# Grouping the sampled tokens' state updates by array rows, and moving one gate product and the later weight casts, in a two-layer hybrid decoder

## Chip, cores and metric

One Trainium2 chip, one core. The metric is the device time of one launch in microseconds (us), as the median of several runs. The launch computes the whole model step.

## The reference

Two decoder layers, float32, over 512 prompt tokens and 8 samples of 4 tokens (544 token columns), model width 1024. Each layer is a half-step SwiGLU FFN, a mixer, cross attention and a second FFN. The mixer is what the change touches. It projects the normalised input once and feeds two groups of heads: sliding-window attention (8 query heads, 2 key heads) and gated linear attention (GLA; 4 heads, key width 64, value width 128). Cut to GLA:

```python
def step(S, inp):                       # one chunk of 64 tokens (4 for a sample)
    b = cumsum(gate); b_last = b[-1]
    q_t, k_t = q * exp(b), k * exp(-b)
    o = q_t @ S + where(causal, q_t @ k_t.T, 0) @ v
    S_new = exp(b_last)[:, None] * S + (k * exp(b_last - b)).T @ v
# per head: rms_norm(o) * silu(g), g one more block of the projection
mix = concat(window_attention, gla) @ w_out
```

The 8 samples each have a state of 4 x 64 x 128 that is read, updated by `S_new`, and written out.

## The kernel before

Tokens lie along the free axis: every activation is 128 features by 544 tokens. A product with a 1024-wide weight block ("block") takes a slab of 128x1024 from HBM into `raw` (3 buffers), and `weights` (L209) splits it into `hi`, a cast on ScalarE (L213), and `lo`, a subtraction on VectorE (L214); `hi` has 3 buffers, `lo` 2. `product` (L221) then issues 48 matmuls at L230 into one of two `pm` tiles of two PSUM banks. All other PSUM results share four one-bank `pa` tiles (`psa`).

The mixer (L676) is a set of Python generators, and the string `MIX` (L52) lists in what order they are advanced, one part at a time. The tile framework then orders the instructions of each engine itself: the place in `MIX` is a priority, and an instruction whose inputs and tiles are there may go earlier. All DMAs are issued by SyncE (SP), in order. Names in `MIX`:

- `rot 0..4`: key and query blocks of the window attention. Part 1 is the block and `taken` (L406), which copies the result (L409) and squares it (L410) into a temporary `u` (3 buffers). Part 2 swaps partition halves by four DMAs into a `z` (L987) and rotates it on VectorE (L988 to L990).
- `qf`: `row_sums` (L264) of the four query squares: matmuls at L272, copies to a `z` at L275, transposes at L278; then the query factors (L258 to L261), which the softmax exponentials (L578) need.
- `gla 0..3`: 128 prompt tokens each. Part 1 makes scores and states, part 2 the outputs (L863 to L873), part 3 is `normed` (L794): squares with sums (L801), square root (L805, "root" below), reciprocal, two products (L809), four transposes (L814) and the copy to `bt` (L815).
- `glas`: the same for the samples. `states`: their state updates. For two samples at a time it masks `kst` (32 sample tokens by 256) into `kdm` (L943, [32, 256]), multiplies `kdm` with the values `vgs` (L948, 32 rows of the array, 64 of its columns), and adds the decayed state (L954); four parts.
- `gated 0..3`: the gate blocks; part 1 the block and its scaling into a `z` (L388), part 2 `silu` (L1028) and product with `bt` (L1029). `bparts` splits the gated result for the output blocks `out 1 x`; `out 0 x` uses the window attention.
- `score n w`, `vals n`, `swas`: window attention. `sv`: its value block.

`z` has 6 buffers (`ATT`, L47), shared by all of these. The order of `MIX` around the change is, before:

```python
"... rot 4, glas, states, rot 3, gla 3, rot 4, gla 3, qf, qf, score 1 0, states, score 0 0, gated 0, sv, "
"score 1 0, states, score 0 1, score 1 1, score 1 0, gated 2, score 0 0, ... gated 1, ... gated 3, ..."
```

Of the kernel before, what the change touches and what calls it, by code (L numbers as in the profile page):

```python
# [7 lines left out]
F32 = mybir.dt.float32  # L8
# [11 lines left out]
NB = 8  # L20
# [33 lines left out]
    "rot 0, gate, key 0, query 1, value 2, query 0, key 1, qdecay 1, value 3, kdecay 1, value 3, kdecay 1, kdecay "  # L54
    "0, sv, value 2, value 0, rot 0, kdecay 0, qdecay 0, value 1, value 0, value 1, gla 0, gla 1, glas, gla 0, "
    "gla 1, gla 2, rot 1, gla 0, gla 2, glas, rot 2, gla 1, gated 0, gla 3, rot 2, rot 1, rot 3, gla 2, rot 4, "
    "glas, states, rot 3, gla 3, rot 4, gla 3, qf, qf, score 1 0, states, score 0 0, gated 0, sv, score 1 0, "
# [5 lines left out]
)  # L63
CROSS = (
    "keys, xq 0, keys, keys, xq 1, xq 2, xq 3, factors, mvalues, mvalues, score 0, xbd, score 1, mvalues, "
# [19 lines left out]
def decoder_kernel(  # L85
# [87 lines left out]
    def hv(t):  # L173
        return t.rearrange("p (a n) -> p a n", a=2)

    fetched = []

    def load(l, i):
        raw = wp.tile([128, 1024], F32, tag="raw", bufs=BUFS["raw"], name="raw")
# [29 lines left out]
    def weights(l, i):  # L209
        raw = ready.pop(0) if ready else load(l, i)  # L210
        hi = wp.tile([128, 1024], F32R, tag="hi", bufs=BUFS["hi"], name="hi")
        lo = wp.tile([128, 1024], F32R, tag="lo", bufs=BUFS["lo"], name="lo")
        act.copy(out=hi, in_=raw)  # L213
        dve.tensor_tensor(out=lo, in0=raw, in1=hi.bitcast(F32), op=ALU.subtract)  # L214
        return hi, lo

    def split(src, hi, lo):
# [185 lines left out]
    def halves():  # L403
        return [slice(0, HN), slice(HN, N)]

    def taken(ps, g, dst):  # L406

        sq = tmp("u")
        act.activation(out=hv(dst), in_=ps[:, :, :HN], func=AF.Copy, scale=g)  # L409
        act.activation(out=hv(sq), in_=ps[:, :, :HN], func=AF.Square)  # L410
        return sq
# [269 lines left out]
    def mixer(l, nx, nxt):  # L681
# [21 lines left out]
        qk = big()  # L703
        q_t, k_t = [qk[:, 0, :], qk[:, 1, :]], [qk[:, 2, :], qk[:, 3, :]]
        ktok = lay.tile([128, 4, 256], F32, tag="ktok", name="ktok")
        kst = lay.tile([32, 256], F32, tag="w1", name="kst")
        ends = lay.tile([128, 2, 16], F32, tag="ends", name="ends")
        def key(i):
            block(2 + i, k_t[i])
# [33 lines left out]

        vg = big()
        vgt = vg.rearrange("p a b -> p (a b)")[:, 0:2048].rearrange("p (n h c) -> p n h c", n=4, h=4)
        vgs = lay.tile([32, 4, 128], F32, tag="vgs", name="vgs")
        def value(h):
            z = tmp("z")
            block(4 + h, z)
            yield 1  # L750
            ps = psa()
            for n in range(4):
                pe.transpose(ps[:, n * 128:n * 128 + 128], z[:, n * 128:n * 128 + 128], ident)
            act.copy(out=vgt[:, :, h, :], in_=ps.rearrange("p (n c) -> p n c", n=4))
            ps = psa()
            pe.transpose(ps[0:32, 0:128], z[:, T:N], ident)
            act.copy(out=vgs[:, h, :], in_=ps[0:32, 0:128])

        def query_decay(i):
            e = tmp("u")  # L760
# [3 lines left out]
        def key_decay(i):  # L764
            e, d = tmp("u"), tmp("u")
            c = cum[i]
            cp, cs = c[:, 0:T].rearrange("p (c t) -> p c t", t=64), c[:, T:N].rearrange("p (c t) -> p c t", t=NT)
            dve.tensor_tensor(
                out=d[:, 0:T].rearrange("p (c t) -> p c t", t=64), in0=cp,
                in1=cp[:, :, 63:64].to_broadcast([128, 8, 64]), op=ALU.subtract,  # L770
            )
            dve.tensor_tensor(
                out=d[:, T:N].rearrange("p (c t) -> p c t", t=NT), in0=cs,
                in1=cs[:, :, NT - 1:NT].to_broadcast([128, NB, NT]), op=ALU.subtract,
            )
            act.activation(out=d, in_=d, func=AF.Exp, scale=-1.0 / 16)
            act.activation(out=ends[:, i, 0:8].unsqueeze(2), in_=cp[:, :, 63:64], func=AF.Exp, scale=1.0 / 16)
            act.activation(out=ends[:, i, 8:16].unsqueeze(2), in_=cs[:, :, NT - 1:NT], func=AF.Exp, scale=1.0 / 16)
            dve.tensor_tensor(out=d, in0=d, in1=k_t[i], op=ALU.mult)
            act.activation(out=e, in_=c, func=AF.Exp, scale=-1.0 / 16)  # L780
            dve.tensor_tensor(out=k_t[i], in0=k_t[i], in1=e, op=ALU.mult)
            yield 1
            ps = psa()
            for n in range(4):
                pe.transpose(ps[:, n * 128:n * 128 + 128], d[:, n * 128:n * 128 + 128], ident)
            act.copy(out=ktok[:, :, i * 128:i * 128 + 128], in_=ps.rearrange("p (n c) -> p n c", n=4))
            ps = psa()
            pe.transpose(ps[0:32, 0:128], d[:, T:N], ident)
            act.copy(out=kst[:, i * 128:i * 128 + 128], in_=ps[0:32, 0:128])

        bt = big()
        gain = col[:, l, C_ON:C_ON + 1]
# [1 line left out]
        def normed(os, c0):  # L794

            sm = smp.tile([128, 4, 4], F32, tag="sm", name="sm")
            su = sm[:, 0, :]
            z = tmp("z")[:, 0:T].rearrange("p (i e v) -> p e i v", e=2, i=2)
            for e in range(2):
                for i in range(2):  # L800
                    act.activation(  # L801
                        out=z[:, e, i, :], in_=os[e][:, i, :], func=AF.Square,
                        accum_out=su[:, 2 * i + e:2 * i + e + 1],
                    )
            act.activation(out=su, in_=su, func=AF.Sqrt, scale=1.0 / 128, bias=eps)  # L805
            dve.reciprocal(out=su, in_=su)
            f = su.rearrange("p (i e) -> p e i", e=2)
            for e in range(2):
                dve.tensor_tensor(  # L809
                    out=z[:, e], in0=os[e], in1=f[:, e].unsqueeze(2).to_broadcast([128, 2, 128]), op=ALU.mult  # L810
                )
            ps = psa().rearrange("p (h t) -> p h t", h=4)
            for h in range(4):
                pe.transpose(ps[:, h, :], z[:, h % 2, h // 2, :], ident)  # L814
            act.activation(out=bt[:, :, c0:c0 + 128], in_=ps, func=AF.Copy, scale=gain)  # L815
# [65 lines left out]
        def gla_sample():  # L881
            sv = s0[l].rearrange("b (i h) d v -> (h d) b i v", i=2)
            st0 = []
            for g in range(2):
                t = cache().rearrange("p (b i v) -> p b i v", b=4, i=2)
                for i in range(2):
                    nc.sync.dma_start(out=t[:, :, i, :], in_=sv[:, 4 * g:4 * g + 4, i, :])
                st0.append(t)
# [18 lines left out]
            for h in range(4):  # L907
                r = slice(32 * h, 32 * h + 32)
                pe.matmul(
                    o[r, :], ams[:, 2 * (h % 2) + h // 2, :], vgs[:, h, :], start=True, stop=False,  # L910
                    tile_position=(0, 32 * h),
                )
            for b in range(NB):
# [20 lines left out]
        def gla_states():  # L934
            st0 = held["st0"]
            osv = o_ss[l].rearrange("b (i h) d v -> (h d) b i v", i=2)
            for b in range(0, NB, 2):
                if b:
                    yield 1
                up = psa().rearrange("p (b i v) -> p b i v", b=2, i=2)  # L940
                for e in range(2):
                    kdm = lay.tile([32, 256], F32, tag="kdm", name="kdm")
                    dve.tensor_scalar(  # L943
                        out=kdm, in0=kst, scalar1=kc[0:32, K_BAT + b + e:K_BAT + b + e + 1], scalar2=None, op0=ALU.mult
                    )
                    for h in range(4):
                        rows = slice(64 * (h % 2), 64 * (h % 2) + 64)
                        pe.matmul(  # L948
                            up[rows, e, h // 2, :], kdm[:, 64 * h:64 * h + 64], vgs[:, h, :], start=True, stop=True
                        )  # L950
                for e in range(2):
                    for i in range(2):
                        t = st0[b // 4][:, (b + e) % 4, i, :]
                        dve.scalar_tensor_tensor(  # L954
                            out=t, in0=t, scalar=ends[:, i, 8 + b + e:9 + b + e], in1=up[:, e, i, :],
                            op0=ALU.mult, op1=ALU.add,
                        )
            for g in range(2):
                for i in range(2):
                    nc.sync.dma_start(out=osv[:, 4 * g:4 * g + 4, i, :], in_=st0[g][:, :, i, :])  # L960
# [6 lines left out]
        def rotated(i):  # L967
            dst = kt if i == 0 else qt[:, i - 1, :]
            g = col[:, l, C_KN:C_KN + 1] if i == 0 else col[:, l, C_QN:C_QN + 1]
            sq = taken(raw_block(8 + i), g, dst)  # L970
            if i == 0:
                ps = psa()[:, 0:10].rearrange("p (b h) -> p b h", b=5)
                by_token(ps, 0, sq, sum_k)
# [75 lines left out]
        def output(half, q):  # L1049
            hh, hl = ((ah, al), (bh, bl))[half]  # L1050
            hi, lo = weights(l, SL_OUT + 4 * half + q)
            for i in range(2):
# [7 lines left out]
                ])  # L1060
                residual(ps, 2 * q + i, 1.0, None if half else nxt)

        run(MIX, dict(
            key=key, gate=gate, query=query, value=value, qdecay=query_decay, kdecay=key_decay, gla=gla_prompt,
            glas=gla_sample, states=gla_states, rot=rotated, qf=query_factors, sv=swa_value, gated=gated,
# [448 lines left out]
```

## Time and profile before

| | us |
|---|---|
| median of 3 runs | 2187.13 (2184.15 to 2187.5) |
| the profiled execution | 2186.87 |
| its span, first to last instruction | 2184.7 |
| TensorE busy in the span | 2165.0 (99%) |
| VectorE busy | 1566.5 (72%) |
| ScalarE busy | 1048.0 (48%) |

The span is what the trace covers; the time has 2.17 us around it. The profile is read by engine: PE is TensorE's matmuls, DVE VectorE, ACT ScalarE, SPq SyncE's queue of DMA issues. The two layers run the same program with other weights; the first layer's mixer runs from about 365 to 617 us, the second's lies 1080 us later.

### The profile page before, as it was taken

Reading aid. Unit: us, or ns where it says so; the run is one execution under the profiler, and the core shown is the slowest. Engines: PE = TensorE matmul, PEld = TensorE weight load, DVE = VectorE, ACT = ScalarE, POOL = GpSimd, SP = SyncE. Lnnn points to the kernel's source line nnn. Section 1 sums busy time; section 2 is a strip of 40 time slices with the busy share of each in tenths; the row PEclk is TensorE's granted clock in tenths of the full one; section 3 lists DMA queues with packets and bytes.
Section 4 is the critical chain, followed back from the end, with each engine's and each line's share of the span. In section 5 each row is a group of like instructions: output and inputs, shape, how many; then the busy total and the mean of one; then the engine's idle time right before and its main releaser. Section 6 shows DMA issues by size and latency. Waiting matters only on the chain.

```text
span 2184.7 us, 40872 instructions
## 1 busy us (share of the span) xinstructions
PE 2165.0 (99%) x17306; PEld 2092.8 (96%) x17306; DVE 1566.5 (72%) x2471; ACT 1048.0 (48%) x1721; POOL 7.0 (0%) x17
## 2 busy tenths in 40 slices
PE   9999999999999999999999999999999999999999
PEld 9999999997897999999999999999879979999999
DVE  6986876547754898777688787765477458977774
ACT  6544443536455644444454444445455466444441
POOL 0000000000000000000000000000000000000000
PEclk9999999999999999999999999999999999999999
DMA  4323333222345232232233323332232533233232
GB/s 141 110 93 98 116 97 130 88 86 73 96 134 195 85 111 96 87 109 95 78 97 99 105 88 92 104 129 90 74 91 88 202 118 105 90 109 93 87 107 71
DMA packets 74998, 227.07 MB, mean 104 GB/s; under 512 B 7712, under 2 KB 19744, under 8 KB 73504
## 3 DMA queue, kind: packets, MB, share of 16 engines
q1 hardware_dynamic: 74816, 224.47, 32.1%
q8 instruction: 135, 2.21, 0.4%
q14 instruction: 47, 0.39, 0.1%
HBM read 214.64 MB, written 9.04 MB: 102 GB/s over the span
## 4 chain that ended last, share of the span: by engine, by line
PE 94%; DVE 3%; DMA 2%; ACT 1%; issue 0%; SPq 0%; ACTq 0%; DVEq 0%
PE pm L230 47%; PE pa L461 36%; PE pa L230 1%; PE pm L1152 1%; PE pm L1114 1%; PE pa L1254 1%; PE pa L1284 1%; PE pm L1237 0%; DMA raw<-in_wts_dram 0%; PE pa L606 0%; PE pm L556 0%; PE pa L239 0%; DMA big<-in_cmv_dram 0%; PE pa L590 0%; PE pa L272 0%; DVE big L219 0%
## 5 line engine op out<-in xcount | busy, mean ns | idle before, releaser
L230 PE MATMUL pm<-big,hi 128*128 128x272 f32 x5632 | 781.3, 290 | 3.4 <-DVE big L219 0.8
L230 PEld LDWEIGHTS pm<-big,hi 128*128 128x128 f32 x5632 | 733.7, 189 | 12.1 <-issue 2.9
L230 PE MATMUL pm<-big,lo 128*128 128x272 f32 x2816 | 410.4, 289 | 0.0
L230 PEld LDWEIGHTS pm<-big,lo 128*128 128x128 f32 x2816 | 374.5, 188 | 2.1 <-issue 1.2
L213 ACT CAST hi<-raw 128x1024 fp32r<-128x1024 f32 x196 | 205.5, 1048 | 241.5 <-PE pm L230 133.0
L214 DVE TENSOR_TENSOR lo<-raw,hi 128x1024 fp32r<-128x1024 f32 x196 | 238.5, 1217 | 51.4 <-PE pm L230 29.7
L218 ACT CAST hs<-sum 128x1024 fp32r<-128x1024 f32 x152 | 160.0, 1053 | 172.1 <-PE pa L461 125.3
L461 PE MATMUL pa<-t,hs 128*128 128x272 f32 x1368 | 238.6, 288 | 0.0
L461 PE MATMUL pa<-big,hs 128*128 128x272 f32 x1064 | 211.2, 288 | 0.1
L461 PEld LDWEIGHTS pa<-t,hs 128*128 128x128 f32 x1368 | 200.9, 188 | 0.0
L219 DVE TENSOR_TENSOR ls<-sum,hs 128x1024 fp32r<-128x1024 f32 x152 | 185.1, 1218 | 1.9 <-ACT hs L218 1.0
L461 PE MATMUL pa<-big,hi 128*128 128x272 f32 x1216 | 178.9, 289 | 0.0
L399 DVE SCALAR_TENSOR_TENSOR x<-pm,x 128x544 f32<-128x544 f32 x192 | 138.1, 719 | 48.1 <-PE pm L230 48.0
L461 PEld LDWEIGHTS pa<-big,hs 128*128 128x128 f32 x1064 | 166.5, 188 | 0.4 <-DVE big L219 0.4
L461 PEld LDWEIGHTS pa<-big,hi 128*128 128x128 f32 x1216 | 163.0, 188 | 0.0
L461 PE MATMUL pa<-t,ls 128*128 128x272 f32 x912 | 152.9, 289 | 0.0
L461 PEld LDWEIGHTS pa<-t,ls 128*128 128x128 f32 x912 | 129.7, 188 | 0.0
L218 ACT CAST hi<-raw 128x1024 fp32r<-128x1024 f32 x76 | 80.1, 1054 | 90.2 <-PE pm L230 81.1
L218 ACT CAST hd<-raw 128x512 fp32r<-128x512 f32 x76 | 47.2, 621 | 137.7 <-PE pa L461 127.6
L447 DVE TENSOR_TENSOR sum<-raw 128x512 f32<-128x512 f32 x152 | 98.2, 686 | 18.0 <-DMA raw<-in_wts_dram 17.6
L461 PE MATMUL pa<-big,lo 128*128 128x272 f32 x608 | 109.6, 288 | 0.0
L447 DVE TENSOR_TENSOR sum<-sum,raw 128x512 f32<-128x512 f32 x152 | 103.9, 684 | 0.0
(306 smaller groups left out, 2611.2 us busy)
## 6 DMA issues: line engine op xcount, KB each, us to landing
raw<-in_wts_dram SPq DMA_DIRECT2D x348, 512.0 KB
big<-in_cmk_t_dram SPq DMA_DIRECT2D x8, 1024.0 KB
big<-in_cmv_dram SPq DMA_DIRECT2D x8, 1024.0 KB
kc<-in_consts_dram SPq DMA_DIRECT2D x2, 1546.0 KB
x<-in_x_dram SPq DMA_DIRECT2D x8, 272.0 KB
z<-big SPq DMA_DIRECT2D x32, 68.0 KB
out_dram<-x SPq DMA_DIRECT2D x8, 272.0 KB
cache<-in_s_dram SPq DMA_DIRECT2D x8, 256.0 KB
```

The costliest lines, as they stand in the source:

```text
L213: act.copy(out=hi, in_=raw)
L214: dve.tensor_tensor(out=lo, in0=raw, in1=hi.bitcast(F32), op=ALU.subtract)
L218: act.copy(out=hi, in_=src)
L219: dve.tensor_tensor(out=lo, in0=src, in1=hi.bitcast(F32), op=ALU.subtract)
L230: pe.matmul(half_of(ps, h, s.stop - s.start), w, x[:, s], start=i == 0, stop=i == len(steps) - 1)
L399: dve.scalar_tensor_tensor(out=x, in0=p, scalar=scale, in1=x, op0=ALU.mult, op1=ALU.add)
L447: dve.tensor_tensor(out=t[:, e], in0=t[:, 0] if x is None else x, in1=y, op=ALU.add)
L461: pe.matmul(ps, u, v, start=first and i == 0, stop=i == len(steps) - 1, skip_group_check=not first)
L1114: pe.matmul(pk[:, h, :], w[:, o:o + 128], x[:, k, :], start=st and h % 2 == 0, stop=sp and h % 2 == 1)
L1152: pe.matmul(pv[:, c, :], x[:, k, c * 128:c * 128 + 128], w[:, o], start=st, stop=sp)
L1254: pe.matmul(o[:, h * 128:h * 128 + 128], held["mv"][:, c, h * 128:h * 128 + 128], pts[:, (2 * e + c) * 128:(2 * e + c + 1) * 128], start=c ...
L1284: pe.matmul(o[32 * e:32 * e + 32, :], pts[:, (2 * g + c) * 128 + 32 * e:(2 * g + c) * 128 + 32 * e + 32], vt[e // 2][:, e % 2, c, :], star ...
```

## The change

- `kst` and `vgs` get 128 rows. SBUF-to-SBUF DMAs copy their 32 rows to the other three groups of 32 rows (six DMAs a layer), and `own_tok`, loaded by four small DMAs a layer, has in row group j the mask of samples j and j+4.
- `states` masks twice instead of eight times, all four row groups at once, into a `z`; its 32 products are the same but lie in four row groups of the array; it has two parts instead of four, and holds two `pa` tiles in each.
- In `MIX`, `gated 2`'s block goes in ahead of the third part of `gla 3`; `gated 1` and `gated 3` each move up one place; `rot 3` and `rot 4`'s second parts come after `gla 3`; `bparts` comes earlier.
- `rot 4`'s square goes into a `z` instead of a `u`.
- `weights` issues the casts of every slab that is traced after `gla 3`'s third part behind that part's root (ACT) and second product (DVE). The edge orders instructions within an engine and adds no semaphore.

```diff
-    "glas, states, rot 3, gla 3, rot 4, gla 3, qf, qf, score 1 0, states, score 0 0, gated 0, sv, score 1 0, "
-    "states, score 0 1, score 1 1, score 1 0, gated 2, score 0 0, score 0 1, score 0 0, score 2 0, score 0 1, "
-    "score 1 1, vals 0, swas, gated 1, score 2 1, score 1 1, gated 1, gated 2, gated 3, score 3 1, vals 1, score "
-    "3 1, score 2 0, score 2 1, score 2 1, states, swas, score 2 0, bparts, vals 2, bparts, score 3 0, score 3 0, "
-    "bparts, gated 3, bparts, out 1 3, out 1 3, out 1 0, swas, ...
+    "glas, gla 3, states, gated 2, gla 3, rot 3, rot 4, qf, qf, score 1 0, score 0 0, gated 0, sv, score 1 0, states, "
+    "score 0 1, score 1 1, score 1 0, gated 1, score 0 0, score 0 1, score 0 0, score 2 0, score 0 1, score 1 1, vals "
+    "0, swas, gated 3, score 2 1, score 1 1, gated 1, gated 2, gated 3, score 3 1, vals 1, score 3 1, bparts, score 2 "
+    "0, bparts, score 2 1, score 2 1, bparts, swas, score 2 0, bparts, vals 2, out 1 3, score 3 0, score 3 0, out 1 "
+    "3, out 1 0, swas, ...
...
-    fetched = []
+    fetched, fence = [], []
...
-        act.copy(out=hi, in_=raw)
-        dve.tensor_tensor(out=lo, in0=raw, in1=hi.bitcast(F32), op=ALU.subtract)
+        with ExitStack() as behind:
+            for ins in fence:
+                behind.enter_context(tc.issue_after(ins))
+            act.copy(out=hi, in_=raw)
+            dve.tensor_tensor(out=lo, in0=raw, in1=hi.bitcast(F32), op=ALU.subtract)
...
-    def taken(ps, g, dst):
-        sq = tmp("u")
+    def taken(ps, g, dst, tag="u"):
+        sq = tmp(tag)
...
-        kst = lay.tile([32, 256], F32, tag="w1", name="kst")
+        kst = lay.tile([128, 256], F32, tag="w1", name="kst")
...
-        vgs = lay.tile([32, 4, 128], F32, tag="vgs", name="vgs")
+        vgs = lay.tile([128, 4, 128], F32, tag="vgs", name="vgs")
+        own_tok = lay.tile([128, 2], F32, tag="own", name="own_tok")
+        for j in range(4):
+            nc.sync.dma_start(out=own_tok[32 * j:32 * j + 32, :], in_=consts[0:32, K_BAT + j:K_BAT + NB:4])
...
-            act.activation(out=su, in_=su, func=AF.Sqrt, scale=1.0 / 128, bias=eps)
+            root = act.activation(out=su, in_=su, func=AF.Sqrt, scale=1.0 / 128, bias=eps)
...
-                dve.tensor_tensor(
+                mult = dve.tensor_tensor(
...
+            if c0 == 384:
+                fence[:] = [root.ins, mult.ins]
...
+            for j in range(1, 4):
+                own = slice(32 * j, 32 * j + 32)
+                nc.sync.dma_start(out=kst[own, :], in_=kst[0:32, :])
+                nc.sync.dma_start(out=vgs[own, :, :], in_=vgs[0:32, :, :])
...
-            for b in range(0, NB, 2):
-                if b:
+            z = tmp("z")
+            kdm = [z[:, 256 * g:256 * g + 256] for g in range(2)]
+            for g in range(2):
+                dve.tensor_scalar(
+                    out=kdm[g], in0=kst, scalar1=own_tok[:, g:g + 1], scalar2=None, op0=ALU.mult
+                )
+            for j0 in (0, 2):
+                if j0:
                     yield 1
-                up = psa().rearrange("p (b i v) -> p b i v", b=2, i=2)
-                for e in range(2):
-                    kdm = lay.tile([32, 256], F32, tag="kdm", name="kdm")
...
+                up = [psa().rearrange("p (g i v) -> p g i v", g=2, i=2) for _ in range(2)]
+                for g in range(2):
+                    for i in range(2):
+                        for j, u in enumerate(up, start=j0):
+                            own = slice(32 * j, 32 * j + 32)
+                            for e in range(2):
+                                h = 2 * i + e
+                                pe.matmul(
+                                    u[64 * e:64 * e + 64, g, i, :], kdm[g][own, 64 * h:64 * h + 64], vgs[own, h, :],
+                                    start=True, stop=True,
+                                )
+                for j, u in enumerate(up, start=j0):
+                    for g in range(2):
+                        for i in range(2):
+                            t = st0[g][:, j, i, :]
...
-            sq = taken(raw_block(8 + i), g, dst)
+            sq = taken(raw_block(8 + i), g, dst, "z" if i == 4 else "u")
...
+        fence[:] = []
         run(MIX, dict(
```

## Rows read from the trace of the kernel before

**Rows 1.** The page, its first line and part 1, the line of PE.

```profile
span 2184.7 us, 40872 instructions
...
PE 2165.0 (99%) x17306; PEld 2092.8 (96%) x17306; DVE 1566.5 (72%) x2471; ACT 1048.0 (48%) x1721; POOL 7.0 (0%) x17
```

**Rows 2.** Waits of PE, whole span: us in total, times, longest.

```profile
PE pa L814 <- DVE z L809: 4.3, 2, 2.1
...
PE pa L272 <- ACT u L410: 1.5, 1, 1.5
```

**Rows 3.** Windows: length, busy us (instructions) by engine, clock, DMA share, GB/s.

```profile
509.74:524.32 14.58, 11.00 (x109) 6.70 (x107) 10.24 (x21) 7.20 (x21) 0.00 (x0) 1.00 0.22 61
...
1589.71:1604.32 14.61, 12.46 (x108) 7.41 (x106) 10.23 (x21) 7.19 (x21) 0.00 (x0) 0.88 0.22 59
...
1596.40:1599.16 2.76, 2.76 (x17) 0.98 (x17) 2.76 (x9) 0.69 (x1) 0.00 (x0) 0.66 0.03 6
```

**Rows 4.** Timeline of PE, first layer: start, us, instruction, [idle before <- releaser].

```profile
513.63 0.65 PE L948 MATMUL pa<-vgs,kdm 32*64 32x128 f32 x8
516.39 0.30 PE L814 MATMUL pa<-ident,z 128*128 128x128 f32 x1 [2.10 <-DVE z L809]
...
520.50 1.10 PE L272 MATMUL pa<-u,kc 128*32 128x272 f32 x4 [1.48 <-ACT u L410]
521.53 1.58 PE L556 MATMUL pm<-kt,big 64*128 64x128 f32 x16
523.04 0.77 PE L278 MATMUL pa<-ident,z 128*128 128x128 f32 x5
```

**Rows 5.** Timelines of ACT and DVE in the same stretch.

```profile
512.69 0.28 ACT L801 ACTIVATE z<-pa 128x128 f32<-128x128 f32 x1 [1.78 <-PE pa L873]
...
513.86 0.30 ACT L805 ACTIVATE sm<-sm,eps 128x4 f32<-128x4 f32 x1
...
519.82 0.62 ACT L410 ACTIVATE u<-pm 128x544 f32<-128x544 f32 x1
...
515.82 0.75 DVE L809 TENSOR_TENSOR z<-pa,sm 128x256 f32<-128x256 f32 x2
```

**Rows 6.** Chain that ended last, first layer's mixer: start, us on the chain, instructions.

```profile
547.51 6.05 PE pm L230 x48
...
523.81 0.58 PE pa L948 x8
...
483.73 0.60 PE pa L839 x16
```

**Rows 7.** Timeline of DVE, first layer: masks, state updates, and gated 0's second part.

```profile
454.62 0.33 DVE L943 TENSOR_SCALAR kdm<-kst,kc 32x256 f32<-32x256 f32 x1
...
519.63 0.70 DVE L1029 TENSOR_TENSOR big<-z,big 128x544 f32<-128x544 f32 x1
...
528.34 1.12 DVE L954 SCALAR_TENSOR_TENSOR cache<-cache,ends,pa 128x128 f32<-128x128 f32 x4 [0.98 <-PE pa L948]
```

**Rows 8.** Timelines of SP and ACT: rot 4's swap; the last copy to vgs.

```profile
510.68 2.42 SPq L987 DMA_DIRECT2D z<-big  x4
...
463.91 0.25 ACT L757 COPY vgs<-pa 32x128 f32<-32x128 f32 x1
```

**Rows 9.** Timelines of ACT, DVE and PE in the score stage, first layer.

```profile
494.08 1.28 ACT L1028 ACT_TABLE_LOAD   x1
...
551.57 1.05 ACT L213 CAST hi<-raw 128x1024 fp32r<-128x1024 f32 x1 [3.63 <-PE pm L230]
...
553.59 0.73 DVE L388 TENSOR_TENSOR z<-pm,r 128x544 f32<-128x544 f32 x1 [2.03 <-PE pm L230]
...
591.52 0.29 DVE L219 TENSOR_TENSOR big<-pa,big 64x128 fp32r<-64x128 f32 x1 [0.33 <-ACT big L218]
...
559.71 0.52 PE L230 MATMUL pm<-big,hi 128*128 128x272 f32 x2 [0.20 <-DVE big L219]
...
593.16 2.05 PE L230 MATMUL pm<-big,hi 128*128 128x272 f32 x15
```

More of the change, by code (lines that the diff above doesn't have):

```diff
@@ L756, in value @@
             pe.transpose(ps[0:32, 0:128], z[:, T:N], ident)
-            act.copy(out=vgs[:, h, :], in_=ps[0:32, 0:128])
+            act.copy(out=vgs[0:32, h, :], in_=ps[0:32, 0:128])
         def query_decay(i):
@@ L788, in key_decay @@
             pe.transpose(ps[0:32, 0:128], d[:, T:N], ident)
-            act.copy(out=kst[:, i * 128:i * 128 + 128], in_=ps[0:32, 0:128])
+            act.copy(out=kst[0:32, i * 128:i * 128 + 128], in_=ps[0:32, 0:128])
         bt = big()
@@ L909, in gla_sample @@
                 pe.matmul(
-                    o[r, :], ams[:, 2 * (h % 2) + h // 2, :], vgs[:, h, :], start=True, stop=False,
+                    o[r, :], ams[:, 2 * (h % 2) + h // 2, :], vgs[0:32, h, :], start=True, stop=False,
                     tile_position=(0, 32 * h),
@@ L936, in gla_states @@
             osv = o_ss[l].rearrange("b (i h) d v -> (h d) b i v", i=2)
-            for b in range(0, NB, 2):
-                if b:
-                    yield 1
-                up = psa().rearrange("p (b i v) -> p b i v", b=2, i=2)
-                for e in range(2):
-                    kdm = lay.tile([32, 256], F32, tag="kdm", name="kdm")
[L943 to L951, printed above, removed]
-                    for i in range(2):
[L953 to L957, printed above, removed]
+            z = tmp("z")
@@ new lines, in gla_states @@
+            kdm = [z[:, 256 * g:256 * g + 256] for g in range(2)]
[5 more added lines that the diff above has]
+                if j0:
+                    yield 1
+                up = [psa().rearrange("p (g i v) -> p g i v", g=2, i=2) for _ in range(2)]
+                for g in range(2):
+                    for i in range(2):
+                        for j, u in enumerate(up, start=j0):
[10 more added lines that the diff above has]
+                            t = st0[g][:, j, i, :]
+                            b = 8 + 4 * g + j
+                            dve.scalar_tensor_tensor(
+                                out=t, in0=t, scalar=ends[:, i, b:b + 1], in1=u[:, g, i, :], op0=ALU.mult, op1=ALU.add
+                            )
```

4 rows, old and new, of the table MIX are left out of this document.

## Prediction

> **What bounds the kernel now.** I read the page first: TensorE is busy for 2165.0 of 2184.7 us [rows 1], so nothing but its own work and its 20 us of idle time can move the end. The waits of PE say where that idle time is: the largest entry is the transposes at L814 waiting for the product at L809, 4.3 us in two waits, and the matmuls at L272 wait 1.5 us for the square at L410 [rows 2]. Both fall in one stretch of the mixer. The windows show it: 14.58 us in the first layer with 11.00 us of matmuls, so 3.58 us idle [rows 3]. The second layer takes 14.61 us for the same instructions and is busy 12.46 us, at a granted clock of 0.88 on the mean: there, matmuls after the first gap run at 0.66 [rows 3], between the two levels of 1.2 and 2.4 GHz, and fill the place of the second gap. Both layers end alike, so I count the same loss for each.
>
> The timelines tell why. The next block is not yet in its order: after the second group of state products at 513.63 it has nothing that is ready, waits 2.10 us until L814, and 1.48 us more before the last four instructions of L272 [rows 4]. Meanwhile ACT squares (L801) from 512.69, takes the root at 513.86, and DVE multiplies at 515.82, which no matmul covers [rows 5]. The square of rot 4 comes only at 519.82 [rows 5], though its block had ended by 509.74, where the window [rows 3] starts: the three `u` buffers hold the squares of rot 1 to 3 until L272 has read them.
>
> **The change part by part.** All sums are per layer, then doubled.
>
> *Gate product at the last turning.* A block is 48 matmuls in 6.05 us on the chain [rows 6]. `gated 2`'s goes between gla 3's outputs and its transposes. From its first square at 512.69 the normed chain needs until 516.57 [rows 5], 4 us; 1.2 us of state products and 6.05 us of block cover that. The 2.10 us wait goes. What is late next is L275's copies, then the query factors.
>
> *Rot 4's square in a `z`.* It then follows its block's copy at L409 directly, around 511, instead of at 519.82. The 1.48 us go. Together 3.58 us.
>
> *State products.* Before: 8 groups a layer, each of 8 instructions in 0.58 us on the chain, 4.64 us. These 64 instructions use the first 32 rows only and two column halves. Afterwards four tiles of the array take turns. The nearest row is L839, two row halves by two column halves and also 128 columns: 16 in 0.60 us, 37.5 ns each [rows 6]. So 64 x 37.5 ns = 2.40 us, a gain of 2.24 us. Bounds: no gain (73 ns as now) and 1.6 us for all (an estimate, a third below L839; gain 3.0 us). I take L839's, whose pattern is the same.
>
> First comes what bears on this from DVE: the state updates at L954 are 16 a layer before and after, four in 1.12 us, and one group of them waited 0.98 us for PE, not the reverse [rows 7]. So PE's time counts here. The Trainium skill, TensorEngine Tiling (Array Packing), section PSUM Bottleneck, speaks against a gain: tiling speeds the matmuls but not the emptying of PSUM. By that rule the sum would lack the 4.48 us of both layers. The trace so far is on the other side.
>
> *Masks.* Eight DVE instructions of 0.33 us become two [rows 7]: 2.0 us of DVE less, worth nothing, as PE waits for neither. Each part now holds two of four `pa` tiles and 8 updates stand in one row on DVE (2.2 us) ahead of L809. The block covers that: 516.6 becomes at most 518.8, against about 519.3 for the block's end. If the cover were gone, it would cost up to 2.2 us.
>
> *DMAs.* Six copies a layer of 32 or 64 KB and four loads of the mask. The nearest row is the swap of rot 4, four issues of 68 KB in 2.42 us of SP [rows 8], so 6 us of SP's queue a layer. They wait for the copies to `vgs`, the last at 463.91 [rows 8], and are needed at 512: 48 us of cover. Behind them on SP stand slab loads, three buffers ahead, and none of PE's larger waits is for a slab [rows 2]. Cost 0; uncovered up to 6 us.
>
> *The edge in `weights`.* `gated 1`'s casts now come after the root (514) and L809 (at most 518.8). Its block starts behind the row sums, about 524: 5 us of cover for 2.3 us of casts. Cost 0; without cover, 2.3 us.
>
> *What follows.* L278 stood at 523.04. The idle 3.58 us go and the block of 6.05 us comes ahead of it. The 32 score instructions (L556) of the stretch now come behind the row sums in `MIX`; the last 16 take 1.58 us [rows 4], so all some 3.2 us. That makes 523.04 - 3.58 + 6.05 - 3.2 = 522.3, with the block already done. The score stage then has one block less to fill gaps. Already before, out 1's first product waited 0.20 us for the last split [rows 9]. Lower bound of what returns: 0; upper: all of the removed 3.58 us. I take 0.5 us a layer, near the row.
>
> **Sum.** 2 x (-3.58 - 2.24 + 0.5) = -10.64 us on the profiled execution's 2186.87 gives 2176.2. It lies 0.26 us below the median of the runs, so 2176.5 for a median.
>
> **Rivals.**
>
> *The score stage keeps its length.* From L278 (523.04) to the last split for out 0 (591.52) it takes 68.5 us; out 0 starts at 593.16, 1.3 us after the split ends (591.81) [rows 4, 9]. If ACT's and DVE's chain sets it, the gain a layer is 0.7 us (L278 earlier) and 1.3 us of slack, 4.1 in all: 2183.0 (2187.13 less 4.1). For it: ACT's exponentials come in bursts; a silu may go as soon as its input is there, with a table load of 1.28 us, as gated 0's did at 494.08 [rows 9], and `gated 2`'s input is now there before the factors' root. Against it: late in the stage ACT idles 3.63 us and DVE 2.03 us waiting for PE's blocks [rows 9], so the chain is held by PE and shrinks when a block leaves.
>
> *Emptying PSUM sets the states' pace*, the rule above: 2181.0 with the other terms as they are. Against it stands the DVE wait [rows 7].
>
> *The change doesn't do what it says.* The order is a priority: the first mask ran at 454.62, some 55 us ahead of its products [rows 7]. If `gated 2`'s matmuls fill earlier places, PE is empty again at the turning, the 2.10 us stay, and 2 x (-1.48 - 2.24) gives 2179.7.
>
> *Slower: the `z` buffers run out.* Six serve all. New tenants are the masks, rot 4's square and `gated 2`'s result, beside sv's and gated 0's, which live until L1029 at 519.63 and beyond [rows 7]. Then normed's `z`, rot 3's and rot 4's swaps and L275's copy pass one after another through the one buffer left. A swap holds it some 6 us, an estimate: 2.42 of issue [rows 8], landing, and three DVE products like L1029's of 0.70 [rows 7]; two of them after L814 (about 519.7) put L275 at 532 instead of 522. It decides when the factors come over 6 us late, as the remaining blocks (two, 12 us) then run out before the first softmax. With 10 us late, less some 2 us of slack, each layer ends 8 us later than before: 2203. Against it: rot 4's swap, the last, was issued at 510.68 [rows 8], ahead of the crowding, and normed's buffer comes free with L814, just before L275 needs one.
>
> **How the numbers follow.** About 0.2% (4.4 us) is what a measurement of this kernel can tell from no change: 2182.7 to 2191.5. Forecast 0.55 (2174 to 2180), score stage 0.18, PSUM 0.07, order 0.09, buffers 0.11. Of the score stage's 0.18, which lies on the edge, 0.03 is faster, 0.13 within and 0.02 slower; of the buffers' 0.11, 0.02 is within and 0.09 slower. So faster 0.55 + 0.07 + 0.09 + 0.03 = 0.74, same 0.13 + 0.02 = 0.15, slower 0.02 + 0.09 = 0.11. The lower end of the range is all gains at their bounds, 2 x (3.58 + 3.0 + 0.2) = 13.6 under the median: 2173.5. The upper end takes in the score stage with 2.5 us more given back: 2185.5. Outside stay the buffers and little else.
>
> **What would show it.** Right: no wait of L814 for L809 and none of L272 for L410; L410 right behind L409; a block between L873 and L814; 64 state products a layer in about 2.4 us; clock 1.00 in the second layer's stretch. Wrong: waits of PE at L590, at L219 or at L272 for ACT's z in the score stage; SP held at L987 for over 5 us with slab loads behind it; a Silu table load ahead of L259; PE's busy time down by less than 4 us though L948 shrank.

## The result, and the profile after

The changed kernel takes 2204.6 us in the median of 5 runs (2203.98 to 2206.81), the one before 2184.15 (2181.43 to 2187.5): a ratio of 1.0095 [1.0084, 1.0107], 20 us slower. The forecast was 2176.5. The rival "the `z` buffers run out", with 2203, is what happened.

The page after, answering to [rows 1]: TensorE is busy as long as before, but the span is 18.1 us longer, so its idle time went from 19.7 to 38.8 us.

```profile
span 2202.8 us, 40882 instructions
...
PE 2164.0 (98%) x17306; PEld 2093.9 (95%) x17306; DVE 1564.6 (71%) x2459; ACT 1053.7 (48%) x1725; POOL 7.0 (0%) x17
```

PE's largest waits after (us in total, times, longest) answer to [rows 2]. The two entries of before have shrunk or gone (L823 is the old L814); their place is taken by L281 (the old L278) for the factor copies, by L967 for the factors' sums, by L593 and L233 for the first softmax. Nearly all are in the score stage or just ahead of it.

```profile
PE pa L281 <- ACT z L278: 5.7, 2, 3.5
PE pa L967 <- DVE inv L261: 4.9, 2, 3.0
PE pa L593 <- DVE sm L587: 4.3, 1, 4.3
PE pm L233 <- ACT s L564: 4.2, 1, 4.2
PE pm L233 <- DVE x L400: 2.9, 6, 0.8
PE pa L823 <- DVE z L816: 2.3, 1, 2.3
```

The windows (columns as in [rows 3]) of the first layer, 520 to 560 us, before and after: 9 us less work of PE in the same 40 us, and a granted clock of 0.74.

```profile
520.00:560.00 40.00, 39.31 (x319) 32.22 (x320) 31.84 (x79) 26.42 (x64) 0.00 (x0) 1.00 0.27 81
```

```profile
520.00:560.00 40.00, 30.35 (x224) 25.43 (x220) 28.55 (x70) 23.25 (x61) 0.00 (x0) 0.74 0.41 121
```

SP's timeline after answers to [rows 8]. Both swaps, eight issues, go out at 522.12, behind two slab loads; before, rot 4's went at 510.68. The queue had stood since 504.54. SP's own waits give 15.9 us of that to the slab loads, which wait for `lo` (L217) to be done with a `raw`; the swaps come behind them in SP's order. The loads cost the swaps little, though: in the run without the edge (below) they are through by 519.74, and the swap then still waits 1.6 us for the reader of normed's `z`, L823.

```profile
504.15 0.39 SPq L866 DMA_DIRECT2D out_dram<-state  x1
520.56 1.46 SPq L180 DMA_DIRECT2D raw<-in_wts_dram  x2
522.12 5.55 SPq L1008 DMA_DIRECT2D z<-big  x8
```

The timelines of ACT, DVE and PE show what hung on that. DVE writes the masks into a `z` at 504.03, ACT rot 4's square into another at 508.21, as planned. The factor copies (L278) come at 524.74, behind a product that frees a gate block's `z`. DVE waits 2.86 us for the swaps' data, the factors' root comes at 529.77, the first exponential at 535.03 (before: 528.66). Rot 4's block ended 2.35 us earlier than before (507.39 against 509.74), so counted from there the copies are 5.9 us late and the first exponential 8.7. PE is idle 3.52, 1.93 and 4.20 us and works at half clock in between: the window from 529.72 to 532.54 has a granted clock of 0.50, the level of 1.2 GHz. The third gap is the block's at L233: it needs a `pm` tile, both hold scores, and ACT empties one of them (L564) only behind the first exponentials in its order.

```profile
508.21 0.62 ACT L413 ACTIVATE z<-pm 128x544 f32<-128x544 f32 x1
...
515.89 0.30 ACT L812 ACTIVATE sm<-sm,eps 128x4 f32<-128x4 f32 x1
...
524.74 0.67 ACT L278 COPY z<-pa 128x272 f32<-128x272 f32 x2 [2.20 <-DVE big L1050]
...
529.77 0.33 ACT L262 ACTIVATE inv<-inv,eps 128x40 f32<-128x40 f32 x1 [3.06 <-DVE inv L261]
...
535.03 0.49 ACT L581 ACTIVATE s<-s,sm,inv 128x128 f32<-128x128 f32 x1
...
539.05 0.56 ACT L564 COPY s<-pm 128x512 f32<-128x512 f32 x1
```

The first exponential in ACT's timeline of before:

```profile
528.66 0.49 ACT L578 ACTIVATE s<-s,sm,inv 128x128 f32<-128x128 f32 x1
```

DVE's and PE's timelines after:

```profile
504.03 0.61 DVE L953 TENSOR_SCALAR z<-kst,own_tok 128x256 f32<-128x256 f32 x2
...
528.20 0.73 DVE L1009 TENSOR_TENSOR z<-z,kc 128x544 f32<-128x544 f32 x1 [2.86 <-DMA z<-big]
```

```profile
514.60 1.11 PE L967 MATMUL pa<-vgs,z 32*64 32x128 f32 x32
515.64 1.14 PE L233 MATMUL pm<-big,lo 128*128 128x272 f32 x7
...
525.18 1.33 PE L281 MATMUL pa<-ident,z 128*128 128x128 f32 x5 [3.52 <-ACT z L278]
...
529.72 2.89 PE L967 MATMUL pa<-vgs,z 32*64 32x128 f32 x32 [1.93 <-DVE inv L261]
...
539.67 1.95 PE L233 MATMUL pm<-big,hi 128*128 128x272 f32 x7 [4.20 <-ACT s L564]
```

### The profile page after: what moved, and what is told of

It is laid out like the page before. It is cut to its first block, busy times and chain, and to the rows that moved or that the text cites. A ratio compares the mean times of both kernels' runs of the same rounds, so it can differ in the third digit from the quotient of the medians.

```text
span 2202.8 us, 40882 instructions
## 1 busy us (share of the span) xinstructions
PE 2164.0 (98%) x17306; PEld 2093.9 (95%) x17306; DVE 1564.6 (71%) x2459; ACT 1053.7 (48%) x1725; POOL 7.0 (0%) x17
## 4 chain that ended last, share of the span: by engine, by line
PE 92%; DVE 4%; ACT 3%; DMA 1%; issue 0%; SPq 0%; DVEq 0%; ACTq 0%
PE pm L233 46%; PE pa L464 36%; PE pm L1174 1%; PE pm L1136 1%; PE pa L233 1%; ACT s L581 1%; PE pa L1276 1%; PE pa L1306 1%; DMA raw<-in_wts_dram 0%; PE pa L609 0%; DVE lo L217 0%; PE pa L242 0%; ACT s L1188 0%; PE pa L882 0%; DMA z<-big 0%
## 5 line engine op out<-in xcount | busy, mean ns | idle before, releaser
L233 PE MATMUL pm<-big,hi 128*128 128x272 f32 x5632 | 780.9, 290 | 9.7 <-ACT s L564 4.2
L233 PEld LDWEIGHTS pm<-big,hi 128*128 128x128 f32 x5632 | 735.3, 189 | 17.1 <-ACT s L564 4.9
L233 PE MATMUL pm<-big,lo 128*128 128x272 f32 x2816 | 412.0, 289 | 1.8 <-DVE lo L217 1.8
L233 PEld LDWEIGHTS pm<-big,lo 128*128 128x128 f32 x2816 | 374.6, 188 | 6.2 <-issue 3.1
L217 DVE TENSOR_TENSOR lo<-raw,hi 128x1024 fp32r<-128x1024 f32 x196 | 238.7, 1219 | 49.8 <-PE pm L233 28.5
L450 DVE TENSOR_TENSOR sum<-raw 128x512 f32<-128x512 f32 x152 | 98.2, 686 | 14.8 <-DMA raw<-in_wts_dram 14.7
```

Of the source, the lines that this page charges most:

```text
L233: pe.matmul(half_of(ps, h, s.stop - s.start), w, x[:, s], start=i == 0, stop=i == len(steps) - 1)
L450: dve.tensor_tensor(out=t[:, e], in0=t[:, 0] if x is None else x, in1=y, op=ALU.add)
```

## The experiments

Ratios are against the kernel before, run beside each. Where a kernel gives a tile a place of its own, `s` and `pt` are cut to 512 of 544 columns, which is all that they use, to make room.

**One buffer more.** In the kernel after:

```diff
-ATT = {"cache": 2, "z": 6, "s": 5, "pt": 5}
+ATT = {"cache": 2, "z": 7, "s": 5, "pt": 5}
```

> The changed kernel with seven z buffers instead of six (room for it from s and pt tiles cut to the 512 columns that they use). Theory 1, the z buffers run out: the swaps of rot 3 and rot 4 and the copies at L278 come earlier, PE's waits at L281 and L967 shrink, and at least half of the 20 us returns, 2185 to 2194. Theory 2, the order leaves the score stage without a block to fill its gaps: 2200 or more, the waits move elsewhere. Theory 3, the edge in weights: no change, 2204.

2194.62 us, 1.005 [1.0035, 1.0065]: 10 us back. Rot 3's swap goes at 513.05, rot 4's still only at 524.97 (SP's timeline): a shortage, and of more than one buffer.

```profile
513.05 2.42 SPq L1008 DMA_DIRECT2D z<-big  x4
524.97 3.36 SPq L1008 DMA_DIRECT2D z<-big  x4
```

**The old order with all other parts.** `MIX` of before in the kernel after.

> The changed kernel with the order of the kernel before; row groups, rot 4's square in a z, masks in a z and the edge stay. Theory 1 (buffers): the masks and the square still sit in z buffers, so part of the loss stays, 2188 to 2200. Theory 2 (order): all of the loss goes and the state products' gain shows, 2180. Theory 3 (edge): 2200 or more.

2178.77, 0.9973 [0.9964, 0.9982]. The loss comes in with the order.

**Without the edge.** In `normed`, `fence[:] = [root.ins, mult.ins]` becomes `pass`.

> The changed kernel without the edge that holds later slabs' casts behind gla 3's root. Theory 3 (edge): at least half of the 20 us returns, below 2194. Theories 1 and 2: within 3 us of 2204.6, or slower where casts now run ahead of the root.

2204.6, 1.0096 [1.0081, 1.0111]: the edge neither costs nor brings anything in this order. SP's waits between 495 and 545 us show the longest of the swap's own, once the slab loads ahead of it are through:

```profile
SPq L1008 <- PE pa L823: 1.6, 1, 1.6
```

**Row groups alone.** In the kernel before: the copies, the masks (in a tile of their own) and the two-part `states`, nothing else.

> The kernel before with the row groups alone: copies by DMA, two masks in a tile of their own, 32 products in four row groups, two parts; order, squares and casts as before (s and pt tiles cut to 512 columns to make room). State products from 4.6 to about 2.3 us a layer. If PE's time in that stretch counts as in the sum: 4 to 5 us faster than before, ratio 0.998. If the emptying of PSUM or the two pa tiles at once set the pace: no gain or up to 5 us slower.

2176.54, 0.9964 [0.9952, 0.9977], the fastest of all and 7.7 us under the kernel before; 4.5 were predicted. The groups by line give the state products' busy time over both layers, before (L948) and here (L961): 6.0 us less.

```profile
L948 PE MATMUL pa<-vgs,kdm 32*64 32x128 f32 x128 | 10.4, 280 | 0.0
```

```profile
L961 PE MATMUL pa<-vgs,kdm 32*64 32x128 f32 x128 | 4.4, 274 | 0.0
```

**Two tenants out of `z`.** In the kernel after, masks and glas' normed in tiles of their own:

```diff
-            z = tmp("z")[:, 0:128]
+            z = lay.tile([128, 128], F32, tag="gz", name="gz")
...
-            z = tmp("z")
+            z = lay.tile([128, 512], F32, tag="kdm", name="kdm")
```

> The changed kernel with two tenants taken out of the z buffers: the masks and the samples' small normed tile get tiles of their own (s and pt tiles cut to 512 columns for room). Seven buffers gave 10 us back, with one swap still issued at 524.97. Buffer theory: both swaps now go before 516, another 5 to 10 us return, 2183 to 2190. Order theory (the swaps stand behind the gate block and gla 3 in the order, and the casts ahead of them on DVE): like seven buffers, 2193 to 2197.

2203.08, 1.0086 [1.0068, 1.0104]: next to nothing. The waits of SP's queue name the reader that rot 4's swap waits for: L275, which reads rot 4's square out of a `z`. With rot 3's swap out at 504.84, the second one still waits for that. Here it is the swap that holds the queue, and the slab loads stand behind it until 526.29.

```profile
SPq L1008 <- PE pa L275: 32.4, 2, 17.0
```

ACT's timeline shows a second loss, which becomes possible now: `gated 2`'s silu stands between gla 3's squares and their root. ACT loads the silu's table, waits 6.77 us for the block, and loads the root's table again.

```profile
510.81 1.28 ACT L1049 ACT_TABLE_LOAD   x1
518.86 0.66 ACT L1049 ACTIVATE z<-z 128x544 f32<-128x544 f32 x1 [6.77 <-DVE z L391]
519.54 1.28 ACT L812 ACT_TABLE_LOAD   x1
520.83 0.30 ACT L812 ACTIVATE sm<-sm,eps 128x4 f32<-128x4 f32 x1
```

**Rotations at their old places.** `MIX` of after with "glas, states, rot 3, gla 3, rot 4, gated 2, gla 3, qf" around the turning.

> The changed kernel with rot 3's and rot 4's second parts back at their former places ahead of gla 3's third part, six z buffers as in the change; gated 2's block stays at the turning. Order theory: the swaps get their buffers first, and most of the loss goes, 2175 to 2188. Buffer theory: some other tenant waits instead (normed, gated 2, the copy at L278), 2190 to 2204.

2185.24, 1.001 [1.0, 1.0019]; swaps from 504.73. It regains 19 us.

**Both of these.**

> Both together: masks and the samples' normed tile out of z, and the rotations at their former places, with gated 2's block at the turning. If the moved block does what the sum said, the turning is covered and this is faster than the row groups alone (2176.5): 2168 to 2174. If the moved block itself costs what it covers, because the score stage lacks it later: 2177 to 2185.

2182.08, 0.9991 [0.9982, 1.0001]. L815 still waits 2.3 us a layer for gla 3's products, behind the silu.

**Gate blocks at their old places, rotations late.** `MIX` from "glas" on: "gla 3, states, gla 3, rot 3, rot 4, qf", and the tail of before.

> The changed kernel with the three gate blocks and what follows them at the places of before; the rotations' second parts stay behind gla 3, six z buffers. If the early block is the cost: 2176 to 2182. If the late rotations are: 2190 or more, with PE waiting for L1011 or L278.

2193.68, 1.0042 [1.0026, 1.0058]. Without the gate's `z` the swaps go from 510.41. That is 14.9 us above the old order with all parts (2178.77), where the kernel after is 25.8 above it: the late rotations do more than half of the harm without the moved block.

**One own buffer for the two swaps**, in the kernel after, order and six `z` untouched:

```diff
-ATT = {"cache": 2, "z": 6, "s": 5, "pt": 5}
+ATT = {"cache": 2, "z": 6, "rt": 1, "s": 5, "pt": 5}
...
-            t = tmp("z")
+            t = tmp("rt" if i > 2 else "z")
```

> The changed kernel, order and all, but the swaps of rot 3 and rot 4 get a buffer of their own, so that they need not wait for a z (s and pt tiles cut to 512 columns for room). Buffer theory: rot 3's swap goes at 504 and rot 4's behind it, before 516, and what the late rotations cost (15 to 19 us by the runs with other orders) goes: 2184 to 2190. Order theory: the products of the rotations stay late on DVE whatever the swaps do: 2195 or more.

2178.99, 0.9977 [0.9967, 0.9986]: 25.6 us under the kernel after. The swaps go at 500.85 and 508.05, no wait of L823, L275 or L281 is left, and the first layer's waits of PE from 470 to 640 us are small ones, most of them in the score stage, 5.5 us together. The cut of `s` and `pt` is not what helps: the run of 2203.08 has it as well. The longest waits:

```profile
PE pm L559 <- ACT s L564: 1.0, 1, 1.0
PE pm L233 <- DVE s L570: 1.0, 1, 1.0
PE pa L593 <- ACT s L581: 0.9, 1, 0.9
PE pm L233 <- DVE lo L217: 0.9, 1, 0.9
```

**The old order with that buffer.**

> The kernel after with the order of before and one own buffer for the swaps of rot 3 and rot 4; against the run with the same buffer and the new order (2179.0) it differs by the order alone. Theory A (the moved block gives nothing where the swaps don't wait): within 2.5 us of that run, 2176.5 to 2181.5, with waits of PE at the turning (L823 for L816) where that run has waits in the score stage. Theory B (the moved block is worth its 4 us): 2182 or more.

2178.8, 0.9978 [0.9969, 0.9987], level with the run above, from which it differs by the order alone. Its idle time, in the same stretch, lies mostly at the turning: 2.1 us for rot 4's rotation and 1.0 for the root's products at L823. So the new order moves PE's idle time and does not shorten it.

**The silu behind the query factors' root.** `with tc.issue_after(last[0])` around the silu, `last` being the root at L262. With the swaps' buffer:

> The same, and the silu of the gate blocks issued behind the query factors' root (an order within ACT, like the edge on the casts), so that no silu and no change of table stands between gla 3's squares and the row sums. If the early silu is part of the loss: 4 to 8 us below the run with the swaps' own buffer. If ACT has the time anyway: within 2 us of it.

2179.49, 0.9983 [0.9973, 0.9992]. With the rotations first and the own tiles:

> The kernel with the rotations at their former places and two tenants out of z (2182.1), and the silu of the gate blocks behind the query factors' root. There the trace has gated 2's silu, which waits for gated 2's block, ahead of gla 3's root, so that L815 waits 2.3 us a layer for what the block was to cover. Silu theory: that wait and two table loads a layer go, 2173 to 2178. Score-stage theory (the loss comes later, one block short): 2180 to 2183.

2178.62, 0.9976 [0.9967, 0.9986]: nothing in the first, 3.5 us in the second, where the wait of L815 is gone and waits in the score stage have grown (L225 for s 1.9 us a layer).

**Rot 4's square in a `z`, in the kernel with row groups alone.**

> The kernel before with the row groups alone (2176.5) and rot 4's square in a z. As in the sum, 1.5 us a layer less: 2173.5. If the square's z then keeps a swap waiting, as with the changed kernel at the old order (2178.8): 2177 to 2180.

2177.82, 0.9974 [0.9964, 0.9984]: no gain; the wait for the square becomes one for the rotation at L556, 6.9 us in four waits.

**The gate block moved alone**, in the kernel before:

```diff
-gla 3, rot 4, gla 3, qf
+gla 3, rot 4, gated 2, gla 3, qf
...
-score 1 0, gated 2, score 0 0, score 0 1,
+score 1 0, score 0 0, score 0 1,
```

> The gate block's move alone, in the kernel before: gated 2's block ahead of gla 3's third part, everything else as before, rotations at their old places, masks in their own tile. Theory A (the score stage gives the block's gain back): the waits of L814 for L809 (4.3 us over both layers) are gone, but new waits of the blocks for ACT and DVE in the score stage take their place, and the time is within 3 us of the kernel before, 2181 to 2187. Theory B (the block's gain is real once the swaps have their buffers): 4 us or more faster, 2180 or less.

2197.47, 1.0062 [1.0049, 1.0075]: neither theory; 14 us slower. ACT's timeline shows why the block covers nothing: gla 3's squares stand behind a weight cast that waits 6.76 us for the `hi` buffer that the moved block is reading, and then come the silu and two table loads. L814 waits 3.3 us a layer instead of 2.1.

```profile
515.52 1.05 ACT L213 CAST hi<-raw 128x1024 fp32r<-128x1024 f32 x1 [6.76 <-PE pm L230]
...
517.10 0.28 ACT L801 ACTIVATE z<-pa 128x128 f32<-128x128 f32 x1
...
518.39 1.28 ACT L1028 ACT_TABLE_LOAD   x1
...
520.36 1.28 ACT L805 ACT_TABLE_LOAD   x1
```

**The same with the edge**, as the change has it.

> The moved block in the kernel before, with the edge in weights as well. In the run without it ACT stood 6.76 us (508.77 to 515.52) at a cast of a later slab that waited for the hi buffer which the moved block was reading, with gla 3's squares (517.10) queued behind it. Theory A (that cast ahead of the root is what took the block's gain): the squares come about 511, the wait of L814 for L809 falls from 3.3 to under 1 us a layer, and the time falls by 6 us or more from 2197.5, to 2191 or less. Theory B (the loss lies in the score stage with one block less): the wait at the turning goes, the time stays above 2193.

2201.98, 1.0081 [1.0069, 1.0093]. The cast is gone from that place, but the squares come only 1.3 us earlier: the next instruction in ACT's order, a copy of rot 4's result at L624, waits 6.44 us for the rotation. The theory of the cast falls. The time is the other theory's, but the wait at the turning has not gone (4.8 us over both layers): the silu still stands between squares and root. The larger wait is in the score stage, 12.2 us over both layers. By the times a block waits there for a `pm` tile that L570 reads until 539.56, and L570 for an ACT copy (L569, 538.25) that stands behind exponentials in ACT's order. The matmuls behind that gap run at a granted clock of 0.59. PE's waits, PE's timeline and DVE's:

```profile
PE pm L233 <- DVE sm L587: 12.2, 2, 6.5
...
539.62 6.28 PE L233 MATMUL pm<-big,hi 128*128 128x272 f32 x30 [6.50 <-DVE sm L587]
...
538.84 0.72 DVE L570 COPY_PREDICATED s<-kc,pm 128x512 f32<-128x512 uint32 x1 [0.80 <-ACT s L569]
```

**And the silu behind the factors' root.**

> The same with the gates' silu issued behind the query factors' root. Theory A: the second table load goes from ahead of the roots, 2.6 us a layer less, so 3 to 6 us below the run without it. Theory B: within 2 us of it, as it was within 1 us in the whole change with an own buffer for the swaps.

2180.78, 0.9985 [0.9976, 0.9993]: 21.2 us less than the run without it, far more than either theory gave. The transposes follow the block without a wait, and the copies at L569 now stand ahead of the exponentials (528.38 and 529.12 against 531.00), so that L570 comes early and the block's wait of 6.50 us is 1.49. That is where the traces show most of the difference. PE's timeline and DVE's:

```profile
518.04 1.14 PE L559 MATMUL pm<-kt,big 64*128 64x256 f32 x8 [0.82 <-DVE z L391]
519.11 0.33 PE L819 MATMUL pa<-ident,z 128*128 128x128 f32 x1
...
529.78 5.80 PE L233 MATMUL pm<-big,hi 128*128 128x272 f32 x32 [1.49 <-DVE sm L577]
...
529.00 0.72 DVE L570 COPY_PREDICATED s<-kc,pm 128x512 f32<-128x512 uint32 x1
```

**Row groups, moved block, edge and silu together.**

> Row groups, gated 2's block moved as the change has it, the edge, and the silu behind the factors' root; the rest of the order, rot 4's square in a u and the rotations as before, masks in their own tile. Theory A (the two gains add: 7.5 us of the row groups and 3.1 of the block): 2173.3, at most 2175. Theory B (the score stage gives the second gain back): 2176 to 2180, no faster than the row groups alone (2176.5), with waits of the blocks at L233 for sums and lo in the score stage.

2186.72, 1.0014 [1.0005, 1.0023].

**The same with the block at its old place.**

> The same with gated 2's block at its old place: row groups, edge and silu order alone. Theory A (the block is what brings the 3 us): 2176.5, as the row groups alone, 2 us or more above the run with the block. Theory B (the silu's place is worth it by itself): 2173 to 2175.

2182.32, 0.9989 [0.998, 0.9998]. Neither sum holds. With the edge, the silu's order and a tile of its own for glas' normed, which the run of row groups alone does not have, the time is 5.8 us longer; the moved block adds 4.4. The other way round, the row groups on top of block, edge and silu (2180.78) cost 5.9 us. With the block PE finds the turning covered, and stands 3.25 us a layer later on, where the block that could have filled the time is spent. The first exponential (532.24, without the move 528.26) is not what it waits for, as the next block starts at 532.22. By the times that block waits for a `pm` tile that L570 reads until 532.17, and L570 stands on DVE behind a gated product and the state updates, eight in a row (L976, 2.15 us from 528.53). PE's timeline with the block, and DVE's:

```profile
526.98 1.99 PE L559 MATMUL pm<-kt,big 64*128 64x256 f32 x14
532.22 6.86 PE L233 MATMUL pm<-big,hi 128*128 128x272 f32 x32 [3.25 <-DVE sm L579]
...
531.45 0.71 DVE L570 COPY_PREDICATED s<-kc,pm 128x512 f32<-128x512 uint32 x1
```

The 32 matmuls behind that gap take 6.86 us at a granted clock of 0.50 and then 0.65, against 4.2 to 4.3 at full clock elsewhere (4.29 in the run without the block).

## Why the prediction was wrong

**The step that failed** is the dismissal of the rival of the `z` buffers: "rot 4's swap, the last, was issued at 510.68, ahead of the crowding". That row is of before, where the swaps' places lie ahead of the last turning. The change itself puts them behind it, so they ask for a `z` after the masks, rot 4's square, `gated 2`'s result and normed. It also cut off the second half of the argument, since normed's buffer was then a swap's before it was L278's (the wait of 1.6 us for L823 in the run without the edge). The runs settle it: with one buffer for the two swaps and no other change but the cut of `s` and `pt`, 25.6 us go. The rival's price came out within 2 us, in part by luck, as its terms differ: it had the factor copies at 532, 10 us late, and they came at 524.74, 5.9 us late from rot 4's end; the first exponential was 8.7 us late by that count, and gaps and half clock in the score stage made up the rest. Its place was slightly off too: where two tenants are out of `z`, the swap of rot 4 waits for L275, which reads the square, and not for L823.

**The gate product at the last turning.** The 2.10 us wait goes where nothing else is late: L823 does not wait in the run with the swaps' buffer. But 0.5 us a layer given back was mis-sized. In that run the first layer's waits from 470 to 640 us are 5.5 us; with the old order and the same buffer they are 4.5 us (2.1, 1.0 and four small ones), and the two times are equal. The upper bound that I gave, all of it, is what was measured, by the mechanism of the rival "the score stage keeps its length".

**Cover on ACT.** I said that a block of 6.05 us covers the normed chain of 4 us. It does only if ACT gets to the chain. With the block moved, ACT stood 6 to 7 us in front of the squares or the root, at a cast, a copy or a silu whose data came later. After the copy the block still covered the chain when no silu came in between (the run of 2180.78), and did not when one did, with its two table loads (the run of 2201.98). I had named the silu's early table load in the rivals, but only ahead of the factors. A load takes 1.28 us and the next instruction starts at once. The Trainium skill, ScalarE: Activation LUTs, section "Table sets: the hidden batching unit", says to group calls by table set. The traces agree that mixing costs here: each change of set is a load of 1.28 us, and two stand between squares and root. The runs with the silu held back (nothing, 3.5 and 21.2 us) say that the worth depends on what waits behind the silu.

**State products.** Right in sign, and larger: 6.0 us of busy time in place of 4.48, since the 8 instructions took 0.65 us as a group against 0.58 on the chain, and 32 now take 1.10 us, 34.4 ns each, against the 37.5 that I took. That these 6.0 us make up most of the 7.7 measured is not shown. From the end of rot 4's block to the cross attention's first block the run is 2.1 us shorter than before in the first layer (107.4 to 105.3), and no shorter in the second (106.8 to 106.9): there the wait at the turning, for gla 3's products at L812 by the times, is 3.4 us, with a granted clock of 0.72 about it (1588.65 to 1600.85). PE's timeline:

```profile
1593.21 0.45 PE L817 MATMUL pa<-ident,z 128*128 128x128 f32 x1 [3.42 <-ACT qbd L621]
```

The rest of the difference between the two traces lies outside the mixers, 2 us of it ahead of anything that the change touches; one trace of each cannot tell the kernels from their executions. The rival of emptying PSUM fell: the state products ran in less than half of their time. The rule of the Trainium skill (TensorEngine Tiling (Array Packing), section PSUM Bottleneck) cost nothing measurable in the run with the row groups alone.

**Masks, rot 4's square, edge.** Masks and glas' normed out of `z` together gave 1.5 us, within the noise. The square runs directly behind L412, as predicted, and its 1.48 us wait goes, but in a `z` it holds up a swap. Why it was late before was read only in part: a `u` came free with the first twelve matmuls of L272 at 518.34, and the square, at 519.82, then stood behind copies on ACT (L621, until 519.19). The edge: 0, as said.

**The sum.** From 2184.2: row groups with masks and square in `z`, in the old order, -5.4; new order where the swaps have a buffer, +0.2; swaps behind four new tenants, +25.6; edge 0: 2204.6. By the places in the trace, the stretch from the end of rot 4's block to the cross attention's first block is 11.9 us longer in the first layer (107.4 to 119.3) and 14.7 in the second (106.8 to 121.5). The rest is 8.4 us shorter: 2.4 ahead of rot 4's end in the first layer, there by 75 us, before anything that the change touches; 1.0 and 3.8 in the two cross attentions, in the second with a DMA wait of before (2.3 us at L1284) that is absent; and small differences. None of it is shown to be the change's.

**Still open.** Which of the edge, the silu's order and glas' own tile costs the 5.8 us on top of the row groups was not separated. Nor is it shown where the row groups' 7.7 us lie, or why moving the block alone loses 14 us in all: the wait at the turning grew by only 2.3 us over both layers, and the rest is spread over small waits and a granted clock of 0.91 in the first layer's 520 to 560 us.

## What to carry to other kernels

Before moving a step later, list the buffers of its pool in the order in which they will be asked for after the move; a row of before tells nothing about an instruction whose place the change moves. Cover on one engine has to be checked on the engine that needs covering: look at what stands in front of the chain in its order, and when that gets its data. A block moved into an idle gap was here taken from a later gap, so price the gap that it leaves as well, and look at what stands ahead of the instruction that empties the PSUM tile of the next block. Gains did not add: alone the row groups gained most (7.7 us) and the moved block with edge and silu order 3.1 (2180.78 against 2183.91 beside it), and together they lost (2186.72).

## What was not expected

The 32 state products that take 1.11 us at full clock took 2.89 us in a window with a granted clock of 0.50, in both layers: 2.6 times as long, not 2. Whether all of the extra is the clock's is not shown. An issue order on ACT alone moved the time by 21.2 us, with the same `MIX` and the same work but for six table loads.
